# W_up by seven products, with each chain of added weight blocks spaced two products apart

## The chip, the cores and the metric

The kernel runs on one core of a Trainium2 chip. The metric is device time in microseconds, the median of several runs of the whole program. The engines that matter here: TensorE (PE) multiplies, VectorE (DVE) and ScalarE (ACT) work element by element, GpSimd (POOL) and SyncE (SP) issue transfers.

## The reference

Two layers of an encoder over 512 tokens of 1024 channels in fp32. The second half of each layer, which the change touches, is

```
h = RMSNorm(x)
x = x + W_down relu(W_up h)^2        W_up: 1024 x 4096, W_down: 4096 x 1024
```

The first half (four attention mixers, gates, an output projection "out") is not changed.

## The kernel before

Products are made to fp32 accuracy from pairs: every operand is split into a rounded `hi` (a cast on ACT, L215) and a remainder `lo` (a subtraction on DVE, L216), and three matmuls (hi x hi, hi x lo, lo x hi) are summed in PSUM. So each weight block, once it has landed, goes through a cast on ACT and a pass on DVE before PE can use it.

The MLP is done in four steps, j = 0 to 3, of 1024 hidden columns. `up` makes u = relu(W_up h)^2 for the step from chunks of 384, 384 and 256 columns, with all 512 tokens as moving columns. Only in the first chunk of j = 0 the tokens are taken in two halves of 256, so that the first half can begin when `norm` has only two of its four token tiles ready. `norm` works on tiles of 128 tokens: a root by Newton steps on [128 x 1] columns, two multiplications over 512 channels (`r_raw`), transposes on PE into PSUM banks (`tp`), and from there `h_hi` and `h_lo`.

For j = 0 to 2 W_down is multiplied by the Strassen-Winograd scheme (`add_product`): the operands are cut into 2 x 2 quarters, and seven products of sums of quarters take the place of eight. The sums of u's quarters (`left_sums`) are made on DVE. The sums of weight quarters (`right_sums`) are made by transfers that add into a block already loaded: SP loads `r_raw`, POOL issues a transfer that adds the next quarter from memory. One such block goes through a chain: split it, add to it, split it again. For j = 3 W_down is plain (`add_rows`), in column chunks of 256, 384 and 384, as "out" is.

The order on the engines is made as the program is built: `up` and `add_product` are generators that take turns, and a scheduler then orders each engine's instructions by its own estimates. On the chip each engine runs its list in order, and waits by semaphores. `NLEFT`, `NRIGHT` and `NSPLIT` are the numbers of buffers for the sums of u, for raw weight blocks, and for split ones. "Product 0 to 6" below are the seven products of a block in the order of the source.

Of the kernel before, what the change touches and what calls it, by code (L numbers as in the profile page):

```python
# [10 lines left out]
F32 = mybir.dt.float32  # L11
# [8 lines left out]
P = 128  # L20
S = 512
# [56 lines left out]
NLEFT, NRIGHT, NSPLIT = 8, 6, 2  # L78
# [86 lines left out]
class Net:  # L165
# [158 lines left out]
    def norm(self, pool, X, ms, g, tag="norm_h", bufs=2):  # L324
# [5 lines left out]
        for t in range(NT):  # L330
# [7 lines left out]
            for _ in range(3):  # L338
                stt(w, y, y, vh, op0=ALU.mult, op1=ALU.mult)
                stt(y, w, 1.5, y, op0=ALU.add, op1=ALU.mult)  # L340
            both = pool.tile([P, 2, S], F32, name=tag, tag=tag, bufs=bufs)
            for half in range(2):
                cs = slice(half * S, half * S + S)
                h = both[:, half, :]
                stt(h, X[t][:, cs], y, g[:, cs], op0=ALU.mult, op1=ALU.mult)
                ps = self.sps.tile([P, 4, P], F32, name="tp", tag="s")
                for j in range(4):
                    self.transpose(ps[:, j, :], h[:, j * P:(j + 1) * P])
                self.split(hi[:, half * 4:half * 4 + 4, t * P:(t + 1) * P],
                           lo[:, half * 4:half * 4 + 4, t * P:(t + 1) * P], ps)  # L350
        return hi, lo
# [752 lines left out]
    def up(self, pool, layer, j, u):  # L1104

        nc = self.nc
        for c0, w in self.col_chunks(0, D):
            units = self.chunk(layer, "up", 0, KD, [(j * D + c0, w)])
            tiles = [self.mm.tile([P, S], F32, name="mm", tag="mm") for _ in range(w // P)] if j == 0 and c0 == 0 else None
            if tiles:  # L1110

                for ts in (slice(0, S // 2), slice(S // 2, S)):
                    for f in range(w // P):
                        self.fm_group(tiles[f][:, ts], self.hT, units, f * P, ts)
            for f in range(0, w, P):
                ft = (c0 + f) // P
                if tiles:
                    ps = tiles[f // P]
                else:
                    ps = self.mm.tile([P, S], F32, name="mm", tag="mm")  # L1120
                    self.fm_group(ps, self.hT, units, f)
                r = pool.tile([P, S], F32, name="relu", tag="relu", bufs=2)
                nc.scalar.activation(r, ps, AF.Relu)
                nc.scalar.activation(u[:, ft, :], r, AF.Square)
                yield
# [8 lines left out]
    def left_split(self, pool, src):  # L1134
        hi, lo = (pool.tile([P, KD // 2, S // 2], F32R, name=x, tag="left", bufs=NLEFT) for x in ("l_hi", "l_lo"))
        self.split(hi, lo, src)
        return hi, lo

    def left_sums(self, pool, x, eng):

        h, kh = S // 2, KD // 2
        x11, x12, x21, x22 = x[:, 0:kh, 0:h], x[:, kh:, 0:h], x[:, 0:kh, h:], x[:, kh:, h:]

        put = lambda src: self.left_split(pool, src)

# [12 lines left out]
        yield put(x12)
        yield put(x22)

    def right_sums(self, pool, layer, name, k0):


        nc = self.nc
# [6 lines left out]
        source = lambda off: self.ins["wflat"][off:off + P * kk * n].rearrange("(p k n) -> p k n", p=P, k=kk)  # L1171

        def load(q):
            got = []
            for off in at[q]:
                raw = pool.tile([P, kk, n], F32, name="r_raw", tag="r_raw", bufs=NRIGHT)
                nc.sync.dma_start(raw, source(off))
                got.append(raw)
            return got

        def put(raws):
            got = []
            for raw in raws:
                hi = pool.tile([P, kk, n], F32R, name="r_hi", tag="r_hi", bufs=NSPLIT)
                lo = pool.tile([P, kk, n], F32R, name="r_lo", tag="r_lo", bufs=NSPLIT)
                self.split(hi, lo, raw)
                got += [(hi[:, k, :], lo[:, k, :]) for k in range(kk)]
            return got

        def add(to, q):  # L1190
            for raw, off in zip(to, at[q]):
                nc.gpsimd.dma_start(raw, source(off), accum_op=ALU.add)  # L1192
# [11 lines left out]
        yield put(load((1, 0)))  # L1204
        add(t, (1, 0))
        yield put(t)

    def add_product(self, pool, X, x, layer, name, k0):

        nc = self.nc  # L1210
        n = D // 2
        bank = {}

        def onto(t, nh, ps, op):
            x = X[t][:, nh * n:nh * n + n]
            nc.vector.tensor_tensor(x, x, ps, op=op)

        left, right = self.left_sums(pool, x, nc.vector), self.right_sums(pool, layer, name, k0)
        for p, ((hi, lo), w) in enumerate(zip(left, right)):

            if p in (0, 1):
                bank[p] = [self.sps.tile([P, S], F32, name="u", tag="s") for _ in range(2)]
            ps = bank[p % 2] if p < 5 else [self.mm.tile([P, S], F32, name="mm", tag="mm") for _ in range(2)]
            fresh = p in (0, 1, 5, 6)
            for k, (whi, wlo) in enumerate(w):
                first, end = fresh and k == 0, k == len(w) - 1
                for q in range(2):
                    toks = slice(q * P, (q + 1) * P)
                    for i, (a, b) in enumerate(((hi, whi), (hi, wlo), (lo, whi))):
                        nc.tensor.matmul(ps[q], a[:, k, toks], b, start=first and i == 0, stop=end and i == 2,  # L1230
                                         skip_group_check=True)
                        self.pe(n)
            for q in range(2):
                if p == 0:
                    onto(q, 0, ps[q], ALU.add)
                elif p == 1:
                    onto(2 + q, 1, ps[q], ALU.add)
                elif p == 2:
                    onto(q, 1, ps[q], ALU.subtract)
                elif p == 3:  # L1240
                    onto(q, 1, ps[q], ALU.add)
                elif p == 4:
                    onto(2 + q, 0, ps[q], ALU.add)
                    onto(2 + q, 1, ps[q], ALU.subtract)
                elif p == 5:
                    onto(q, 0, ps[q], ALU.add)
                else:
                    onto(2 + q, 0, ps[q], ALU.add)
            yield

    def run(self):
# [14 lines left out]
        for layer in range(self.depth):  # L1266
            act = self.attention(layer)
            last = layer == self.depth - 1
            with tc.tile_pool(name=f"mlp{layer}", bufs=1) as pool:
# [7 lines left out]
                self.hT = self.norm(pool, X, ms, g, "r_raw", NRIGHT)  # L1277
# [97 lines left out]
```

## Time and profile before

| | |
|---|---|
| median of 3 runs | 1854.19 us (1853.7 to 1855.83) |
| profiled execution | 1853.6 us, its span 1851.7 us, mean granted clock of TensorE 0.988 |
| PE busy | 1787.2 us, 97% of the span |
| DVE busy | 1201.0 us, 65% |
| ACT busy | 935.0 us, 50% |
| POOL busy | 419.0 us, 23% |

The rows below give times from the start of the span. PE's listed durations overlap, since matmuls are pipelined: what one costs is the distance between two starts. In layer 0 the MLP follows the last matmul of "out" at 596 us.

### The profile page before, as it was taken

How to read it: one execution, taken by the hardware profiler on the slowest of the kernel's cores; microseconds unless marked ns; L12 is line 12 of the kernel's file. 1: busy time of each engine (PE TensorE's matmuls, PEld its weight loads, DVE VectorE, ACT ScalarE, POOL GpSimd, SP SyncE). 2: the span in 40 equal slices, each digit the busy share in tenths (PEclk: the TensorE clock that was granted, in tenths of full speed). 3: DMA queues.
4: the chain of work that ended last, by engine and by line, in shares of the span. 5: the costliest groups of instructions: out<-in, count | busy, mean ns of one | idle time of the engine just before them, and what ended most of it. 6: DMA issues, size and time to landing. Idle time of an engine off the chain costs nothing.

```text
span 1851.7 us, 26873 instructions
## 1 busy us (share of the span) xinstructions
PE 1787.2 (97%) x9392; PEld 1556.9 (84%) x9392; DVE 1201.0 (65%) x2553; ACT 935.0 (50%) x1905; POOL 419.0 (23%) x1215
## 2 busy tenths in 40 slices
PE   6998999999999999999999989999999999999999
PEld 5897897887889888888999979887878898888889
DVE  6677876677665465655477878666876664565652
ACT  4565664555533454554346656645553345554541
POOL 2462254333010000010023604532422000010100
PEclk9999999999999999999999989999999999999999
DMA  4312123121324656564343211221222545565622
GB/s 164 115 53 68 60 73 93 44 69 56 90 83 154 207 124 166 129 156 105 96 153 98 76 61 52 79 72 60 73 66 73 159 151 134 149 153 165 138 82 89
DMA packets 73320, 193.91 MB, mean 105 GB/s; under 512 B 8928, under 2 KB 14048, under 8 KB 73184
## 3 DMA queue, kind: packets, MB, share of 16 engines
q1 hardware_dynamic: 66272, 167.02, 28.2%
q0 software_dynamic: 6912, 25.17, 8.0%
q8 instruction: 74, 1.21, 0.3%
q14 instruction: 62, 0.51, 0.1%
HBM read 187.97 MB, written 4.19 MB: 104 GB/s over the span
## 4 chain that ended last, share of the span: by engine, by line
PE 78%; DVE 8%; POOL 6%; issue 3%; ACT 2%; DMA 2%; SPq 1%; POOLq 0%; DVEq 0%; ACTq 0%
PE mm L285 19%; PE mm L286 19%; PE mm L287 19%; PE u L1230 9%; PE mm L1230 4%; PE tp L222 3%; PE s L604 2%; POOL rs_w_qk L235 2%; DVE w_lo L216 1%; POOL rs_y_qk L238 1%; POOL rs_w_qk L236 1%; POOL rs_w_qk L237 1%; PE y L631 1%; PE y L630 1%; DMA x<-in_x 1%
## 5 line engine op out<-in xcount | busy, mean ns | idle before, releaser
L285 PE MATMUL mm<-h_hi,w_hi 128*128 128x512 f32 (+1 forms) x1104 | 424.8, 386 | 1.8 <-DVE sig L1029 1.0
L286 PE MATMUL mm<-h_lo,w_hi 128*128 128x512 f32 (+1 forms) x1104 | 423.5, 385 | 1.7 <-DVE h_lo L216 1.4
L287 PE MATMUL mm<-h_hi,w_lo 128*128 128x512 f32 (+1 forms) x1104 | 419.6, 385 | 4.3 <-DVE w_lo L216 2.4
L216 DVE TENSOR_TENSOR w_lo<-w_raw,w_hi 128x768 fp32r<-128x768 f32 (+2 forms) x337 | 299.8, 899 | 158.5 <-ACT w_hi L215 157.1
L215 ACT CAST w_hi<-w_raw 128x768 fp32r<-128x768 f32 (+2 forms) x337 | 258.1, 774 | 232.2 <-PE mm L286 105.3
L287 PEld LDWEIGHTS mm<-h_hi,w_lo 128*128 128x128 f32 x1104 | 208.5, 189 | 44.7 <-DVE w_lo L216 3.9
L285 PEld LDWEIGHTS mm<-h_hi,w_hi 128*128 128x128 f32 x1104 | 208.6, 189 | 43.1 <-DVE sig L1029 2.9
L286 PEld LDWEIGHTS mm<-h_lo,w_hi 128*128 128x128 f32 x1104 | 209.0, 189 | 41.0 <-DVE h_lo L216 2.5
L287 PE MATMUL mm<-w_hi,h_lo 128*128 128x384 f32 (+1 forms) x576 | 190.0, 331 | 2.6 <-DVE h_lo L216 2.6
L286 PE MATMUL mm<-w_lo,h_hi 128*128 128x384 f32 (+1 forms) x576 | 189.7, 331 | 1.8 <-DVE w_lo L216 1.7
L285 PE MATMUL mm<-w_hi,h_hi 128*128 128x384 f32 (+1 forms) x576 | 189.2, 334 | 1.1 <-ACT w_hi L215 0.5
L216 DVE TENSOR_TENSOR r_lo<-r_raw,r_hi 128x1024 fp32r<-128x1024 f32 x84 | 102.7, 1223 | 130.3 <-ACT r_hi L215 130.3
L1192 POOL DMA_DIRECT2D r_raw<-in_wflat x48 | 41.6, 870 | 613.9 <-DVE r_lo L216 248.9
L235 POOL TENSOR_TENSOR rs_w_qk<-rs_y_qk 128x4 f32<-128x4 f32 (+2 forms) x216 | 61.8, 286 | 436.2 <-DVE rs_y_qk L233 300.0
L215 ACT CAST r_hi<-r_raw 128x1024 fp32r<-128x1024 f32 x84 | 88.3, 1051 | 69.2 <-PE u L1230 39.2
L286 PEld LDWEIGHTS mm<-w_lo,h_hi 128*128 128x128 f32 x576 | 110.4, 192 | 3.5 <-DVE w_lo L216 2.6
L287 PEld LDWEIGHTS mm<-w_hi,h_lo 128*128 128x128 f32 x576 | 110.1, 191 | 3.6 <-DVE h_lo L216 2.9
L285 PEld LDWEIGHTS mm<-w_hi,h_hi 128*128 128x128 f32 x576 | 110.1, 192 | 2.8 <-ACT h_hi L215 0.8
L216 DVE TENSOR_TENSOR pt_lo<-tp,pt_hi 128x256 fp32r<-128x256 f32 (+2 forms) x144 | 77.9, 552 | 39.6 <-ACT pt_hi L215 30.8
L215 ACT CAST pt_hi<-tp 128x256 fp32r<-128x256 f32 (+2 forms) x144 | 66.8, 478 | 66.4 <-PE tp L222 52.5
L1230 PE MATMUL u<-r_hi,l_lo 128*128 128x512 f32 x240 | 93.7, 390 | 0.0
L1230 PE MATMUL u<-r_lo,l_hi 128*128 128x512 f32 x240 | 93.5, 390 | 0.0
(192 smaller groups left out, 3602.5 us busy)
## 6 DMA issues: line engine op xcount, KB each, us to landing
w_raw<-in_wflat SPq DMA_DIRECT2D x248, 384.0 KB, 3.3
r_raw<-in_wflat SPq DMA_DIRECT2D x48, 512.0 KB, 3.6
r_raw<-in_wflat POOLq DMA_DIRECT2D x48, 512.0 KB, 5.8
w_raw<-in_wflat SPq DMA_DIRECT2D x88, 256.0 KB, 2.7
x<-in_x SPq DMA_DIRECT2D x8, 512.0 KB, 5.7
d_full<-in_mask_d SPq DMA_DIRECT2D x8, 448.0 KB, 4.5
x_save<-x SPq DMA_DIRECT2D x4, 512.0 KB, 4.5
x<-x_save SPq DMA_DIRECT2D x4, 512.0 KB, 5.5
```

Of the source, the lines that this page charges most:

```text
L215: self.nc.scalar.copy(hi, src)
L216: self.nc.vector.tensor_tensor(lo, src, hi.bitcast(F32), op=ALU.subtract)
L222: self.nc.tensor.transpose(out, in_, self.ident_r if short else self.ident)
L235: eng.tensor_tensor(w, y, y, op=ALU.mult)
L236: eng.tensor_tensor(w, w, v, op=ALU.mult)
L237: eng.tensor_scalar(w, w, -0.5, 1.5, op0=ALU.mult, op1=ALU.add)
L285: nc.tensor.matmul(ps, st[0], mv[0], start=first, stop=False)
L286: nc.tensor.matmul(ps, st[0], mv[1], start=False, stop=False)
L287: nc.tensor.matmul(ps, st[1], mv[0], start=False, stop=last)
L604: self.nc.tensor.matmul(ps, q[:, qc], k[:, kc], start=i == 0, stop=i == len(ks) - 1)
L1192: nc.gpsimd.dma_start(raw, source(off), accum_op=ALU.add)
L1230: nc.tensor.matmul(ps[q], a[:, k, toks], b, start=first and i == 0, stop=end and i == 2, skip_group_check=True)
```

## The change

W_up is multiplied by seven products too. The first 512 hidden columns are made plainly (`up_first`), all of them in two halves of 256 tokens and from `r_raw` blocks; the other seven blocks of 512 columns of a layer go through the new `up`: seven products of 24 matmuls, each with a stationary 128 x 128 and 256 moving columns. The sums of h's quarters are made once per layer (`row_sums`) from a copy of h that `norm` now keeps (`keep`, eight copies from PSUM on ACT). The sums of weight quarters of a block are one chain of three adding transfers, used in products 0, 2, 4 and 6, and one addition of two loaded blocks on DVE (`merge`). `right_sums` of W_down is put in the same form: three adding transfers for each half and a merge on DVE, in place of four transfers. POOL issues 78 such transfers instead of 48 in all.

u is held in quarter blocks of 4 x 256. `norm` works out the root of the next tile ahead of the transposes of this one. The last product of W_down takes two chunks of 512 columns, from `r_raw` blocks. PE has 10178 matmuls instead of 9314.

```diff
-NLEFT, NRIGHT, NSPLIT = 8, 6, 2
+NLEFT, NRIGHT, NSPLIT, NU = 6, 8, 4, 7
...
-        for t in range(NT):
+        y = inverse(0)
+        for t in range(NT):
             both = pool.tile([P, 2, S], F32, name=tag, tag=tag, bufs=bufs)
...
+            y = inverse(t + 1) if t + 1 < NT else None
+            banks = []
+            for half in range(2):
                 ps = self.sps.tile([P, 4, P], F32, name="tp", tag="s")
...
+            if keep is not None:
+                for half, ps in enumerate(banks):
+                    nc.scalar.copy(keep[half, t // 2][:, :, t % 2 * P:t % 2 * P + P], ps)
...
+    def split_block(self, pool, raw):
+        hi = pool.tile(list(raw.shape), F32R, name="r_hi", tag="r_hi", bufs=NSPLIT)
+        lo = pool.tile(list(raw.shape), F32R, name="r_lo", tag="r_lo", bufs=NSPLIT)
+        self.split(hi, lo, raw)
+        return [(hi[:, k, :], lo[:, k, :]) for k in range(raw.shape[1])]
+
+    def merge(self, to, raw):
+        self.nc.vector.tensor_tensor(to, to, raw, op=ALU.add)
...
+    def up_first(self, pool, layer, u):
+
+        units = self.plain_blocks(pool, layer, "up", 0, 0)
...
+        for f in range(4):
+            self.fm_group(tiles[f][:, early], self.hT, units, f * P, early)
+            self.squared_relu(u[0, 0][:, f, :], tiles[f][:, early])
...
+    def row_sums(self, pool, raw):
...
+        s1 = total(x21, x22, ALU.subtract)
+        hi, lo = (x[:, 0:kh, h:] for x in self.hT)
+        self.split(hi, lo, s1)
+        own = [(hi[:, k, :], lo[:, k, :]) for k in range(kh)]
+        s2 = total(s1, x11, ALU.subtract)
+        sums = [s2, total(x11, x21, ALU.subtract), total(s2, x12, ALU.add)]
...
+        def product(ps, left, raw, fresh):
+            right = self.split_block(pool, raw)
+            for f in range(2):
+                for k, (x, w) in enumerate(zip(left, right)):
+                    for i, (a, b) in enumerate(((1, 0), (0, 0), (0, 1))):
+                        nc.tensor.matmul(ps[:, f, :], w[a][:, f * P:(f + 1) * P], x[b], start=fresh and f + k + i == 0,
+                                         stop=k == kh - 1 and i == 2, skip_group_check=True)
...
+        t = load(0, 0)
+        a = bank()
+        product(a, x11, t, True)
+        add(t, 0, 1)
+        nc.scalar.copy(out[0, 0], a)
+        yield
+        c = bank()
+        product(c, x12, load(1, 0), True)
...
+        b = bank()
+        product(b, s1, t, True)
+        add(t, 1, 1)
+        nc.scalar.copy(out[1, 1], b)
+        t3, w22 = load(0, 1), load(1, 1)
+        self.merge(t3, w22)
+        yield
+        product(b, s4, w22, False)
...
+        product(a, s2, t, False)
+        add(t, 1, 0)
...
+        product(a, s3, t3, False)
...
+        product(a, x22, t, False)
...
         t = load((0, 0))
-        yield put(t)
+        got = put(t)
         add(t, (0, 1))
-        yield put(t)
+        yield got
+        yield put(load((1, 0)))
+        got = put(t)
         add(t, (1, 1))
-        yield put(t)
-        yield put(load((1, 1)))
-        t3 = load((0, 1))
-        add(t3, (1, 1))
+        yield got
+        t3, w22 = load((0, 1)), load((1, 1))
+        for a, b in zip(t3, w22):
+            self.merge(a, b)
+        yield put(w22)
...
+                        for i, _ in enumerate(self.up(pool, layer, j * D + c * S, u, c, sums)):
+                            if prev is not None and (i + c) % 2:
+                                next(prev, None)
```

Where instructions stand now, at three places. First PE at the norm of layer 0, behind the last matmuls of "out" (`m_hi`, `m_lo`); `tp` are the transposes, `mm<-h..` the first matmuls of W_up. Before:

```order
L287 MATMUL mm<-w_hi,m_lo 128x384
L222 MATMUL tp<-ident,r_raw 128x128 x16
L285 MATMUL mm<-h_hi,w_hi 128x256 x3
L286 MATMUL mm<-h_lo,w_hi 128x256
L287 MATMUL mm<-h_hi,w_lo 128x256
```

And now:

```order
L287 MATMUL mm<-w_hi,m_lo 128x384
L222 MATMUL tp<-ident,r_raw 128x128 x32
L285 MATMUL mm<-h_hi,r_hi 128x256
L286 MATMUL mm<-h_lo,r_hi 128x256
L285 MATMUL mm<-h_hi,r_hi 128x256
```

All 32 transposes stand ahead of W_up's first matmul; the other 16 stood among the matmuls before.

Second ACT at the same place. Before, the transposed banks of tiles 2 and 3 (the last four `h_hi`) with the first two raw blocks of W_down among them:

```order
L215 CAST h_hi_6903<-tp_6986 128x4x128
L215 CAST h_hi_6903<-tp_6994 128x4x128
L215 CAST r_hi_7465<-r_raw_7461 128x1024
L215 CAST h_hi_6903<-tp_7018 128x4x128
L215 CAST r_hi_7469<-r_raw_7463 128x1024
L215 CAST h_hi_6903<-tp_7026 128x4x128
```

And now, from the bank after tiles 0 and 1 on; `r_hi_7053` is the first weight block of W_up:

```order
L361 COPY h_raw_6903<-tp_6942 128x4x128
L361 COPY h_raw_6905<-tp_6949 128x4x128
L361 COPY h_raw_6903<-tp_6976 128x4x128
L215 CAST h_hi_6907<-tp_7010 128x4x128
L361 COPY h_raw_6905<-tp_6983 128x4x128
L215 CAST h_hi_6907<-tp_7017 128x4x128
L361 COPY h_raw_6904<-tp_7010 128x4x128
L361 COPY h_raw_6906<-tp_7017 128x4x128
L215 CAST h_hi_6907<-tp_7029 128x4x128
L215 CAST r_hi_7053<-r_raw_7051 128x1024
L215 CAST h_hi_6907<-tp_7036 128x4x128
```

Six copies stand ahead of the last tile's first `h_hi`, and the cast of W_up's first block stands behind that.

Third DVE in j = 0, after the first block of columns. `r_raw_7329` is the block of the chain of the second block (products 0, 2, 4, 6), `r_raw_7558` that of the third. Before, DVE had here the casts of plain chunks:

```order
L216 TENSOR_TENSOR w_lo_7218<-w_raw_7216,w_hi_7217 128x768
L216 TENSOR_TENSOR w_lo_7224<-w_raw_7222,w_hi_7223 128x768
L216 TENSOR_TENSOR w_lo_7230<-w_raw_7228,w_hi_7229 128x768
L216 TENSOR_TENSOR w_lo_7236<-w_raw_7234,w_hi_7235 128x768
L216 TENSOR_TENSOR w_lo_7326<-w_raw_7324,w_hi_7325 128x512
L216 TENSOR_TENSOR l_lo_7458<-u_7035,l_hi_7457 128x1024
```

And now:

```order
L216 TENSOR_TENSOR l_lo_7626<-u_7047,l_hi_7625 128x1024
L216 TENSOR_TENSOR r_lo_7333<-r_raw_7329,r_hi_7332 128x1024
L216 TENSOR_TENSOR r_lo_7366<-r_raw_7363,r_hi_7365 128x1024
L216 TENSOR_TENSOR h_lo_6908<-l_sum_7295,h_hi_6907 128x4x256
L216 TENSOR_TENSOR r_lo_7398<-r_raw_7329,r_hi_7397 128x1024
L216 TENSOR_TENSOR r_lo_7433<-r_raw_7429,r_hi_7432 128x1024
L1228 TENSOR_TENSOR u_7049<-u_7049,mm_7362 128x512
L216 TENSOR_TENSOR r_lo_7462<-r_raw_7329,r_hi_7461 128x1024
L1134 TENSOR_TENSOR r_raw_7702<-r_raw_7702,r_raw_7704 128x1024
L216 TENSOR_TENSOR r_lo_7494<-r_raw_7427,r_hi_7493 128x1024
L216 TENSOR_TENSOR r_lo_7525<-r_raw_7329,r_hi_7524 128x1024
L216 TENSOR_TENSOR r_lo_7562<-r_raw_7558,r_hi_7561 128x1024
```

Four splits of one block now stand in DVE's list with an adding transfer between each two, and the first split of the third block stands behind the last of them.

## Rows read from the trace of the kernel before

**Rows 1.** The page's busy times: engine, busy us, share of span, instructions.

```profile
PE 1787.2 (97%) x9392; PEld 1556.9 (84%) x9392; DVE 1201.0 (65%) x2553; ACT 935.0 (50%) x1905; POOL 419.0 (23%) x1215
```

**Rows 2.** Windows over the MLP of layer 0: length, busy us by engine, clock, transfers.

```profile
core 0: us, PE busy (x) PEld busy (x) DVE busy (x) ACT busy (x) POOL busy (x), PEclk, DMA share, GB/s
...
640.00:706.00 66.00, 66.00 (x292) 54.56 (x292) 40.08 (x43) 32.79 (x41) 3.45 (x4) 1.00 0.45 118
...
809.00:891.00 82.00, 82.00 (x362) 67.82 (x362) 48.67 (x53) 41.09 (x53) 3.45 (x4) 1.00 0.43 110
```

**Rows 3.** PE's timeline at 384 and 256 moving columns: start, us, instruction.

```profile
1505.79 0.33 PE L286 MATMUL mm<-w_lo,m_hi 128*128 128x384 f32 x1
...
1507.00 0.33 PE L287 MATMUL mm<-w_hi,m_lo 128*128 128x384 f32 x1
...
1511.10 0.28 PE L285 MATMUL mm<-h_hi,w_hi 128*128 128x256 f32 x1
...
1514.33 0.28 PE L285 MATMUL mm<-h_hi,w_hi 128*128 128x256 f32 x1
```

**Rows 4.** Timeline of the norm in layer 0, three engines.

```profile
596.03 1.91 PE L222 MATMUL tp<-ident,r_raw 128*128 128x128 f32 x16
...
596.66 2.05 ACT L215 CAST h_hi<-tp 128x512 fp32r<-128x512 f32 x4 [0.64 <-PE tp L222]
597.09 0.55 DVE L1096 TENSOR_TENSOR x<-x,mm 128x384 f32<-128x384 f32 x1
...
597.68 1.88 DVE L216 TENSOR_TENSOR h_lo<-tp,h_hi 128x512 fp32r<-128x512 f32 x3
...
598.28 0.61 PE L285 MATMUL mm<-h_hi,w_hi 128*128 128x256 f32 x3 [0.34 <-ACT h_hi L215]
...
599.61 0.39 PE L286 MATMUL mm<-h_lo,w_hi 128*128 128x256 f32 x1 [0.72 <-DVE h_lo L216]
...
603.56 0.22 DVE L339 SCALAR_TENSOR_TENSOR norm_w<-norm_y,norm_vh 128x1 f32<-128x1 f32 x1
...
604.01 1.42 DVE L345 SCALAR_TENSOR_TENSOR r_raw<-x,norm_y,norm_g 128x512 f32<-128x512 f32 x2
```

**Rows 5.** Groups by form, 600 to 891 us: busy us, mean ns, idle before.

```profile
L216 DVE TENSOR_TENSOR r_lo<-r_raw,r_hi 128x1024 fp32r<-128x1024 f32 x42 | 51.4, 1223 | 64.0 <-ACT r_hi L215 64.0
...
L215 ACT CAST r_hi<-r_raw 128x1024 fp32r<-128x1024 f32 x42 | 44.1, 1051 | 33.5 <-PE u L1230 18.3 <-PE mm L1230 13.0 <-DMA r_raw<-in_wflat 2.1
...
L1216 DVE TENSOR_TENSOR x<-x,u 128x512 f32<-128x512 f32 x36 | 23.4, 682 | 1.6 <-PE u L1230 1.5
```

**Rows 6.** Groups by form, 900 to 1500 us, at 256 columns.

```profile
L216 DVE TENSOR_TENSOR pt_lo<-tp,pt_hi 128x256 fp32r<-128x256 f32 x24 | 10.0, 418 | 2.1 <-ACT pt_hi L215 1.6 <-PE y L630 0.5
...
L215 ACT CAST pt_hi<-tp 128x256 fp32r<-128x256 f32 x24 | 8.9, 371 | 11.6 <-PE tp L222 7.7 <-PE y L631 3.8
```

**Rows 7.** Timeline of DVE and POOL at a link of W_down's chain.

```profile
659.07 1.22 DVE L216 TENSOR_TENSOR r_lo<-r_raw,r_hi 128x1024 fp32r<-128x1024 f32 x1
660.21 1.22 DVE L216 TENSOR_TENSOR l_lo<-l_sum,l_hi 128x1024 fp32r<-128x1024 f32 x1
...
660.59 0.86 POOL L1192 DMA_DIRECT2D r_raw<-in_wflat  x1 [0.87 <-DVE r_lo L216]
```

**Rows 8.** Transfers issued in 650 to 700 us, then in 608 to 640.

```profile
r_raw<-in_wflat POOLq DMA_DIRECT2D x4, 512.0 KB, 5.5
...
r_raw<-in_wflat POOLq DMA_DIRECT2D x4, 512.0 KB, 8.8
```

**Rows 9.** The page's queues: packets, MB, share of 16 engines' span.

```profile
q1 hardware_dynamic: 66272, 167.02, 28.2%
q0 software_dynamic: 6912, 25.17, 8.0%
```

**Rows 10.** A pause of PE in the attention of layer 0: timeline, then a window.

```profile
1068.72 1.29 PE L285 MATMUL mm<-y_hi,w_hi 128*128 128x512 f32 x2 [4.64 <-ACT y_hi L215]
...
1068.72:1072.50 3.78, 3.78 (x9) 2.90 (x10) 3.78 (x15) 1.45 (x3) 0.03 (x1) 0.50 0.23 85
```

More of the change, by code (lines that the diff above doesn't have):

```diff
@@ L1102, in add_rows @@
                     ms[t].append(part)
[L1104 to L1125, printed above, removed]
@@ L1211, in add_product @@
         n = D // 2
+        add, sub = ALU.add, ALU.subtract
+        steps = (("a", True, ((0, 0, add),)), ("c", True, ((0, 0, add),)), ("b", True, ((1, 1, add),)),
+                 ("b", False, ((0, 1, add),)), ("a", False, ((0, 1, sub),)),
+                 ("a", False, ((1, 0, add), (1, 1, sub))), ("c", True, ((1, 0, add),)))
         bank = {}
[L1214 to L1224, printed above, removed]
+        left, right = self.left_sums(pool, x), self.right_sums(pool, layer, name, k0)
+        for (hi, lo), w, (key, fresh, places) in zip(left, right, steps):
+            if fresh:
+                bank[key] = [self.sps.tile([P, S], F32, name="u", tag="s") for _ in range(2)]
+            ps = bank[key]
             for k, (whi, wlo) in enumerate(w):
-                first, end = fresh and k == 0, k == len(w) - 1
                 for q in range(2):
@@ L1229, in add_product @@
                     for i, (a, b) in enumerate(((hi, whi), (hi, wlo), (lo, whi))):
[L1230 to L1231 removed]
+                        nc.tensor.matmul(ps[q], a[:, k, toks], b, start=fresh and k + i == 0,
+                                         stop=k == len(w) - 1 and i == 2, skip_group_check=True)
                         self.pe(n)
[L1233 to L1248, printed above, removed]
+            for th, nh, op in places:
+                for q in range(2):
+                    to = X[2 * th + q][:, nh * n:nh * n + n]
+                    nc.vector.tensor_tensor(to, to, ps[q], op=op)
             yield
@@ L1281, in run @@
                 for j in range(4):
-                    u = pool.tile([P, KD, S], F32, name="u", tag="u", bufs=2)
-                    for i, _ in enumerate(self.up(pool, layer, j, u)):
-                        if prev is not None and (j < 3 or i):
-                            next(prev, None)
+                    u = self.blocks(pool, "u")
+                    if j == 0:
+                        self.up_first(pool, layer, u)
+                        sums = self.row_sums(pool, raw)
+                    for c in range(1 if j == 0 else 0, 2):
+                        for i, _ in enumerate(self.up(pool, layer, j * D + c * S, u, c, sums)):
+                            if prev is not None and (i + c) % 2:
+                                next(prev, None)
                     if j < 3:
```

146 lines of the change are left out of this document (105 added, 41 removed).

## The prediction

> **What bounds the kernel now.** I read the page's busy times first: TensorE works 1787.2 of 1851.7 us, 97% [rows 1], so the end is set by the sum of its work and the few places where it waits. The windows over the MLP come next: in 640 to 706 us it is busy all 66.0 us, in 809 to 891 all 82.0, while VectorE has 61% and 59% of these stretches and ScalarE about 50% [rows 2]. There is nothing to be won in the body of the MLP but fewer or shorter matmuls; and any wait that the change brings shows in full.
>
> The price of a matmul is its spacing, not its listed duration. With 512 moving columns, 82.0 us hold 362 [rows 2]: 0.2265 us. With 256, from 1511.10 to 1514.33 there are 27 steps: 0.1196; with 384, from 1505.79 to 1507.00, seven: 0.173 [rows 3].
>
> The timeline of the norm in layer 0 comes third. After the last matmul of "out" PE makes the 16 transposes of token tiles 0 and 1, and at 598.28 begins on W_up for these 256 tokens, with waits of 0.34 and 0.72 us [rows 4]. The norm of tiles 2 and 3 is worked out under these matmuls. Layer 1 shows the same.
>
> **Term 1, TensorE's work.** Seven of the eight blocks of 512 hidden columns change from 96 matmuls of 512 (96 x 0.2265 = 21.75) to 7 products of 24 matmuls of 256 (168 x 0.1196 = 20.09): -1.65. The saving of an eighth in columns comes out as less than 8% in time, since a 256-column matmul costs more than half of a 512 one. Over 7 blocks and 2 layers: -23.1. The last product of W_down in each layer goes from column chunks of 256, 384, 384 (96 matmuls each: 11.5 + 16.6 + 16.6 = 44.7) to 192 of 512 (43.5): -1.2, twice -2.4. The first block runs in halves throughout (192 x 0.1196 = 23.0 against 17.2 + 5.4 = 22.6): +0.3, twice +0.6. W_down's other products keep their number and their size. Sum -24.9.
>
> Here the Trainium skill is more generous than the rows. TensorE: Matmul & The Clock Gate, Back-to-back issue gap, gives for a single stream N/2.4 + 2.5 ns, 109 ns for 256 columns and 216 for 512; by that an estimate for a block is 18.3 against 20.7 us, and the total would come out some 10 us lower than below. The rows show the two sizes next to this very work, and are taken.
>
> **Term 2, from the norm to the first steady product.** PE's order now has all 32 transposes ahead of the first matmul of W_up, so that matmul waits for the whole norm. I walk layer 0 on the axis of the old trace, since the order up to there is the same.
>
> The last matmul of "out" ends at 596.2. The addition to x for tile 3 then takes 0.55 (596.9; the w_lo casts that delayed it before are gone), two steps of tile 2's root 0.45, its two multiplications 1.42 [rows 4]: 598.7. VectorE next makes six h_lo at 0.63 each (1.88 for three) and six root steps of tile 3, about 0.23 each (603.56 to 604.01 is two) [rows 4]: 5.2 us, and loses about 0.4 because ScalarE now has a copy of h to write for each transposed bank, each behind the h_lo of that bank: 604.3. Half of the multiplications 0.7, four transposes 0.5 (1.91 for 16), h_hi 0.59 [rows 4], and r_hi of the first block, which stands behind it on ScalarE, 1.05 [rows 5]: the first matmul at 607.1, against 598.28.
>
> PE has then 192 matmuls of 256 for the first block, and behind them the products 0, 1, 2, 4, 3 of the second block, before the first product of the third. With no wait that is 37.3 us. VectorE is the one to follow. From 606.1 it has in its order 2 h_lo, 4 r_lo, 4 sums of rows of h, 10 w_lo of 256 columns, a merge, an l_lo and the r_lo of product 0: eleven passes over 1024 columns at 1.14 (659.07 to 660.21 [rows 7]), ten at some 0.4 (0.418 [rows 6]), two at 0.63: 17.8 us. The casts that they follow on ScalarE (0.371 for 256 columns [rows 6]) cost some 1.8 more. r_lo of product 0 is done at 625.7.
>
> From here a chain decides: r_lo, an adding transfer into the same block, r_hi, r_lo. A link in the old trace: r_lo at 659.07 + 1.22, the transfer is issued at 660.59 [rows 7], so 0.3; 5.5 to landing where little else moves [rows 8]; 1.05 and 1.22 for the casts [rows 5]; 8.15 with 0.1 for signals. Little covers it: one product (2.9 us) stands between the uses of the block in products 0 and 2 and none between 2 and 4, because W_down has no product to put there yet. Three links end at 650.2, and behind the third r_lo stands, in VectorE's order, the r_lo for the third block's first product: 651.3. PE begins that product at 651.3. In the old scheme the same work without waits would be reached at 598.28 + 1.1 for the later half of the transposes and the old waits beside them at 0.7 + 0.9, that is 638.4 with its 37.3. So 12.9 per layer, twice +25.8. The bounds: casts at their closest spacing and a link at 7.7 give 10.5 per layer; transfers that land in 8.8 us, as they did where queues were full [rows 8], give 3 x 3.3 more, 22.
>
> **Term 3, the steady part, j = 1 to 3.** PE has 336 matmuls of 256 and 168 of 512: 78.2 us per j. VectorE's passes come to 43 of 1024 columns and 22 of 512 (0.68 [rows 5]): 52.6 + 15 = 67.6 by durations, 64 by spacing: 82 to 86%, against 60% now. The DMA engines: q1 moved 167.02 MB in 28.2% of the span, 1.64 us per block of 512 KB, q0 its 48 additions in 8.0%, 3.1 each [rows 9]; 16 loads and 12 additions per j are 63 of 78 us, 81%. Neither is full, and with W_down's products between those of W_up a link of 8.15 lies under two to four products (5.7 to 14 us). Walking one period in the order of the engines, I find covers of 0.2 us (second half of W_down's third product, whose load waits for an r_lo), 0.7, 1.4 and one of -0.3. I take 1 us per j, between 0 and 4: +6 for six j (0 to +24).
>
> Costed at nothing: the merges (counted in VectorE's load; 1.2 us each on the chain if VectorE should be full), the copies into the output banks (ScalarE at 62%), the u quarter blocks, and the clock. As for the clock: where PE stood still from 1064.1 to 1068.7, the granted clock went to 0.50 (the 1.2 GHz level), and was still there until 1072.5, with 0.42 us per matmul of 512 [rows 10]. The gap of the norm may do the same, which costs up to 1.9 us in the first block, but PE then waits that much less for the chain behind it.
>
> **Sum.** -24.9 + 25.8 + 6 = +6.9 on the profiled execution's 1853.6: 1860.5. The three runs' median lies 0.6 above it: 1861.
>
> **The rivals.**
> Faster. The waits of term 2 stay near 8 us per layer and the steady part has none: -25 + 16 = -9: 1845. For it: VectorE's 17.8 us between the norm and r_lo of product 0 hold most of the delay, and would be shorter if its passes ran closer than in the rows. Against it: three links of transfers are latency, and nothing lies between them. It decides where all new waits fall below 21 us, 10.6 per layer.
> No change to be measured (a run's spread makes 0.2%, 3.7 us, the limit). The walk holds, at its shorter bound, and term 3 is nought to 4: -25 + 22 + 2 = -1: 1853.
> The steady part runs into VectorE or the transfers. For it: 82 to 86% and 81% of load, additions that took 8.8 us to land at 608 to 640 [rows 8]. At 3.3 us more per link and three uncovered links per j, of which half lies in the covers: 5 us per j, 30 in all, on the top of the rest: 1885. Against it: loads go out up to eight blocks ahead.
> The product scheme on W_up gives nothing: a block at 7/8 of the columns but 1.75 times the matmuls would have to space at 0.1295; the 27 steps say 0.1196, so I give that no chance of its own.
>
> **Chances.** My forecast (1858 to 1872) 0.40, the steady part bound (1872 to 1895) 0.18, no change 0.18, faster 0.24. So faster 0.24, same 0.18, slower 0.58. The range leaves out the far ends of the first and the last: 1843 to 1882; the likeliest case alone has 1857 to 1870.
>
> **What would show it.** Matmuls of 256 in W_up at 0.12 us. At each norm a gap on PE of about 7 us besides the transposes, with a granted clock below 1 behind it. Then two waits of 2 to 4 us, both put down to r_lo on VectorE, the second ahead of the third block's first product, and additions on POOL 8 us apart. From then to the end of the layer PE busy to 98% or more, VectorE near 80%. I am wrong in term 2 if the first matmul of W_up begins before 604 or the third block's first product before 647; wrong in term 3 if PE's waits on r_lo come to more than 4 us per j.

## The result

The changed kernel takes 1865.91 us (median of 4 runs, 1864.41 to 1869.67) against 1853.95 for the kernel before in the same measurement: ratio 1.0066, interval 1.0048 to 1.0083. It is slower, as forecast, by 12 us where 7 were forecast; the span of the profiled execution went from 1851.7 to 1862.6 us.

The page's busy times and PE's timeline and windows say where. First the page's busy times after the change (they answer to [rows 1]):

```profile
PE 1772.7 (95%) x10256; PEld 1577.2 (85%) x10256; DVE 1320.9 (71%) x2645; ACT 1010.2 (54%) x1999; POOL 445.2 (24%) x1245
```

PE has 864 matmuls more than before (10256 against 9392 in the traces) and is busy 14.5 us less, yet the span is 10.9 us longer: its idle time grew by 25.4 us. PE's busy time also hides matmuls at half clock, as will be seen.

Next come rows of PE's timeline at the norm of layer 0 (start, us, instruction; they answer to [rows 4]):

```profile
596.94 1.91 PE L222 MATMUL tp<-ident,r_raw 128*128 128x128 f32 x16
600.74 1.33 PE L222 MATMUL tp<-ident,r_raw 128*128 128x128 f32 x8 [1.89 <-ACT h_raw L361]
605.40 1.94 PE L222 MATMUL tp<-ident,r_raw 128*128 128x128 f32 x8 [3.33 <-DVE r_raw L349]
608.10 0.58 PE L285 MATMUL mm<-h_hi,r_hi 128*128 128x256 f32 x1 [0.77 <-ACT r_hi L215]
608.48 0.41 PE L286 MATMUL mm<-h_lo,r_hi 128*128 128x256 f32 x1
608.69 0.41 PE L285 MATMUL mm<-h_hi,r_hi 128*128 128x256 f32 x1
```

W_up begins 11.2 us after the first transpose; before it was 2.25. Three waits stand in between: for a copy of h on ACT (it reads the PSUM bank that the next transposes need), for the last tile's multiplication, and for the cast of the first weight block. The last two matmuls start 0.21 us apart, where 0.12 is the spacing at full clock [rows 3]: half clock, as the windows below show.

After that the chain of adding transfers, in the timelines of ACT, DVE, POOL and PE:

```profile
626.37 1.05 ACT L215 CAST r_hi<-r_raw 128x1024 fp32r<-128x1024 f32 x1 [2.20 <-PE mm_y L286]
627.45 1.23 DVE L216 TENSOR_TENSOR r_lo<-r_raw,r_hi 128x1024 fp32r<-128x1024 f32 x1 [2.03 <-ACT r_hi L215]
629.30 1.02 POOL L1125 DMA_DIRECT2D r_raw<-in_wflat  x1 [110.67 <-DVE r_lo L216]
636.39 1.05 ACT L215 CAST r_hi<-r_raw 128x1024 fp32r<-128x1024 f32 x1 [3.94 <-DMA r_raw<-in_wflat]
639.01 0.87 POOL L1125 DMA_DIRECT2D r_raw<-in_wflat  x1 [8.68 <-DVE r_lo L216]
646.69 0.58 PE L1215 MATMUL mm<-w_hi,r_lo 128*128 128x256 f32 x1 [4.71 <-DVE r_lo L216]
646.93 0.85 POOL L1125 DMA_DIRECT2D r_raw<-in_wflat  x1 [7.06 <-DVE r_lo L216]
655.97 0.38 PE L1215 MATMUL mm<-h_hi,r_lo 128*128 128x256 f32 x1 [1.49 <-DVE r_lo L216]
656.21 0.87 POOL L1125 DMA_DIRECT2D r_raw<-in_wflat  x1 [8.43 <-DVE r_lo L216]
```

POOL's transfers stand 9.7, 7.9 and 9.3 us apart (the last is the next chain's first), and PE waits twice for an r_lo, 4.71 and 1.49 us. ACT's first row shows a wait that the forecast did not have: the cast of product 0's block waits 2.20 us for PE, which still reads the first block from the split buffers. Layer 1 has the same two waits:

```profile
1560.46 0.39 PE L1215 MATMUL mm<-w_hi,r_lo 128*128 128x256 f32 x1 [3.42 <-DVE r_lo L216]
1569.70 0.58 PE L1215 MATMUL mm<-h_hi,r_lo 128*128 128x256 f32 x1 [3.28 <-DVE r_lo L216]
```

The windows (busy us by engine, granted clock, share of the transfer engines; answers to [rows 2, 10]) give the clock behind these gaps, and the steady part:

```profile
606.00:608.00 2.00, 1.34 (x7) 0.93 (x5) 0.69 (x1) 1.48 (x3) 0.00 (x0) 0.50 0.57 121
612.00:616.00 4.00, 4.00 (x31) 4.00 (x31) 4.00 (x5) 0.54 (x2) 0.00 (x0) 0.84 1.03 423
644.00:646.00 2.00, 0.00 (x0) 0.00 (x0) 0.59 (x1) 1.67 (x2) 0.00 (x0) 0.50 0.47 193
650.00:652.00 2.00, 2.00 (x16) 2.00 (x15) 0.00 (x0) 0.00 (x0) 0.00 (x0) 0.79 0.95 197
...
660.00:740.00 80.00, 80.00 (x517) 72.87 (x516) 65.09 (x68) 49.97 (x60) 10.35 (x12) 1.00 0.77 182
740.00:820.00 80.00, 79.97 (x514) 72.64 (x513) 64.10 (x66) 48.33 (x58) 10.53 (x13) 1.00 0.79 187
820.00:890.00 70.00, 70.00 (x455) 64.03 (x454) 56.77 (x58) 45.40 (x55) 9.31 (x11) 1.00 0.83 198
```

From 660 us on PE does not wait at all, with VectorE at 81% and the transfer engines at 77 to 83%. So what the change loses, it loses in some 60 us between the norm and the third block.

### The profile page after: what moved, and what is told of

Same layout as the page of the kernel before. It is cut to its first block, busy times and chain, and to the rows that moved or that the text cites. A ratio compares the mean times of both kernels' runs of the same rounds, so it can differ in the third digit from the quotient of the medians.

```text
span 1862.6 us, 28777 instructions
## 1 busy us (share of the span) xinstructions
PE 1772.7 (95%) x10256; PEld 1577.2 (85%) x10256; DVE 1320.9 (71%) x2645; ACT 1010.2 (54%) x1999; POOL 445.2 (24%) x1245
## 4 chain that ended last, share of the span: by engine, by line
PE 74%; DVE 8%; POOL 7%; issue 4%; DMA 3%; ACT 2%; SPq 0%; POOLq 0%; DVEq 0%; ACTq 0%
PE mm L1215 14%; PE mm L285 14%; PE mm L286 13%; PE mm L287 13%; PE u L1344 12%; PE tp L222 3%; DMA r_raw<-in_wflat 2%; POOL rs_w_qk L235 2%; PE s L615 2%; POOL rs_w_qk L236 1%; POOL rs_w_qk L237 1%; POOL rs_y_qk L238 1%; PE y L642 1%; PE y L641 1%; DVE w_lo L216 1%
## 5 line engine op out<-in xcount | busy, mean ns | idle before, releaser
L216 DVE TENSOR_TENSOR r_lo<-r_raw,r_hi 128x1024 fp32r<-128x1024 f32 x206 | 250.8, 1221 | 101.1 <-ACT r_hi L215 99.4
L215 ACT CAST r_hi<-r_raw 128x1024 fp32r<-128x1024 f32 x206 | 215.7, 1050 | 128.7 <-PE mm L1215 47.9
L285 PE MATMUL mm<-h_hi,w_hi 128*128 128x512 f32 x544 | 217.9, 401 | 1.1 <-DVE sig L1040 1.0
L287 PE MATMUL mm<-h_hi,w_lo 128*128 128x512 f32 x544 | 214.4, 400 | 4.4 <-DVE w_lo L216 2.5
L286 PE MATMUL mm<-h_lo,w_hi 128*128 128x512 f32 x544 | 215.7, 397 | 0.0
L1215 PE MATMUL mm<-h_hi,r_lo 128*128 128x256 f32 x448 | 127.2, 284 | 4.8 <-DVE r_lo L216 4.8
L1215 PE MATMUL mm<-h_lo,r_hi 128*128 128x256 f32 x448 | 128.2, 286 | 0.0
L1215 PE MATMUL mm<-h_hi,r_hi 128*128 128x256 f32 x448 | 128.0, 286 | 0.0
L1344 PE MATMUL u<-r_hi,l_hi 128*128 128x512 f32 x336 | 126.2, 390 | 0.0
L286 PEld LDWEIGHTS mm<-h_lo,w_hi 128*128 128x128 f32 x544 | 103.5, 190 | 20.5
```

What stands on the lines that cost most here:

```text
L215: self.nc.scalar.copy(hi, src)
L216: self.nc.vector.tensor_tensor(lo, src, hi.bitcast(F32), op=ALU.subtract)
L285: nc.tensor.matmul(ps, st[0], mv[0], start=first, stop=False)
L286: nc.tensor.matmul(ps, st[0], mv[1], start=False, stop=False)
L287: nc.tensor.matmul(ps, st[1], mv[0], start=False, stop=last)
L1215: nc.tensor.matmul(ps[:, f, :], w[a][:, f * P:(f + 1) * P], x[b], start=fresh and f + k + i == 0, stop=k == kh - 1 and i == 2, skip_group_ ...
```

## The experiments

The attention phases of these runs, which no experiment touches, differ from profile to profile: what is left of the span without the MLPs and "out" lies between 1071.6 us (before) and 1076.9 (e10). The table therefore also has the MLPs by themselves, from PE's timeline: from the first transpose of the MLP's norm to that of the next norm (layer 0) or to the end (layer 1), summed; and "out", the two output projections, from their first matmul to the MLP's first transpose. Each ratio is to runs of the kernel before in the same measurement, whose medians lay between 1853.95 and 1855.53.

| kernel | median us | ratio to before, 95% interval | MLPs us | "out" us |
|---|---|---|---|---|
| before | 1853.95 | | 685.4 | 94.8 |
| after | 1865.91 | 1.0066 (1.0048 to 1.0083) | 695.4 | 94.4 |
| e1_own_sums | 1850.24 | 0.9976 (0.9967 to 0.9985) | 679.0 | 94.7 |
| e2_early_split | 1851.93 | 0.9979 (0.9970 to 0.9989) | 675.0 | 97.8 |
| e3_both | 1839.12 | 0.9913 (0.9897 to 0.9930) | 663.4 | 98.6 |
| e4_own_sums_more | 1849.92 | 0.9967 (0.9954 to 0.9980) | 678.7 | 94.5 |
| e5_kept_busy | 1861.70 | 1.0040 (1.0025 to 1.0055) | 691.7 | 94.7 |
| e6_kept_less_busy | 1863.31 | 1.0045 (1.0027 to 1.0062) | 697.6 | 94.6 |
| e7_split_in_norm | 1840.87 | 0.9926 (0.9910 to 0.9943) | 669.2 | 94.6 |
| e8_second_block_plain | 1855.97 | 0.9997 (0.9986 to 1.0007) | 683.0 | 96.9 |
| e9_split_one_two | 1839.81 | 0.9917 (0.9904 to 0.9930) | 669.5 | 94.5 |
| e10_split_two_late | 1838.84 | 0.9911 (0.9899 to 0.9924) | 667.1 | 94.3 |
| e11_kept_busy_again | 1863.06 | 1.0048 (1.0036 to 1.0061) | 691.4 | 94.5 |
| e12_kept_less_busy_again | 1865.48 | 1.0057 (1.0045 to 1.0069) | 695.6 | 94.5 |

**e1, the chain on VectorE.** The four weight quarters of the second block (`own` is `j == 0`) are loaded once, and the sums made by `merge`:

```diff
         t = load(0, 0)
+        if own:
+            w = {(1, 0): load(1, 0), (0, 1): load(0, 1), (1, 1): load(1, 1)}
+            load = lambda r, c: w[r, c]
+            add = lambda raw, r, c: self.merge(raw, w[r, c])
         a = bank()
```

> The chain of the second block (j = 0) without adding transfers: its four weight quarters are loaded once and added on VectorE; all else as after the change. Theory A (the forecast's term 2: a chain of transfers is what PE waits for there): the waits on r_lo of 4.7 and 1.5 us vanish, and with them the half clock behind the longer one (some 2.2 us), 8.4 per layer: 1849 us. Rival B (VectorE's list is what limits, the transfers lie beside it): with three more passes on VectorE the wait only moves, 1862 us or more.

1850.24 us, theory A's figure within 1.3; the MLPs lost 16.4 us, 8.2 per layer against 8.4 expected. The list of PE's waits in layer 0 up to 900 us has only those of the norm left:

```profile
PE tp L222 <- DVE r_raw L349: 3.3, 1, 3.3
PE tp L222 <- ACT h_raw L361: 1.9, 1, 1.9
PE mm L285 <- ACT r_hi L215: 0.8, 1, 0.8
```

In layer 1 one wait on r_lo of 1.1 us is left, ahead of the third block's first product. Nothing of the size of rival B appears, and it falls: VectorE had room for three more passes just there, and what PE waited for was the transfers' latency.

**e2, the first weight blocks split early.**

```diff
                 raw = self.blocks(pool, "h_raw")
+                units = self.plain_blocks(pool, layer, "up", 0, 0)
                 self.hT = self.norm(pool, X, ms, g, "r_raw", NRIGHT, raw)
...
-                        self.up_first(pool, layer, u)
+                        self.up_first(pool, layer, u, units)
```

> The first weight blocks of W_up are split ahead of the norm in the program, so that PE's matmuls for the first 256 tokens stand between the transposes again; all else as after the change. Theory A: PE starts near 600 us instead of 608, without half clock; the chain begins some 5 us earlier because four r_lo have left VectorE's list behind the norm: 4 to 6 us per layer, 1854 to 1858 us. Rival B (the gap of the norm is swallowed by the chain behind it, which hangs on the last tile's h and not on PE): 0 to 2 per layer, 1862 to 1866 us.

1851.93 us, below even theory A's range. PE's timeline at the norm has W_up's matmuls between the transposes again, with no wait above 0.84 us, and the two waits of the chain are still there:

```profile
598.36 1.91 PE L222 MATMUL tp<-ident,r_raw 128*128 128x128 f32 x16
601.11 0.62 PE L285 MATMUL mm<-h_hi,r_hi 128*128 128x256 f32 x3 [0.84 <-ACT h_hi L215]
602.16 0.66 PE L222 MATMUL tp<-ident,r_raw 128*128 128x128 f32 x4 [0.32 <-ACT h_raw L361]
...
638.16 0.58 PE L1214 MATMUL mm<-w_hi,r_lo 128*128 128x256 f32 x1 [2.91 <-DVE r_lo L216]
...
647.36 0.39 PE L1214 MATMUL mm<-h_hi,r_lo 128*128 128x256 f32 x1 [0.53 <-DVE r_lo L216]
...
1546.61 0.39 PE L1214 MATMUL mm<-w_hi,r_lo 128*128 128x256 f32 x1 [2.02 <-DVE r_lo L216]
...
1555.91 0.58 PE L1214 MATMUL mm<-h_hi,r_lo 128*128 128x256 f32 x1 [3.33 <-DVE r_lo L216]
```

In layer 0 both are shorter than after the change (4.71 and 1.49), in layer 1 only the first is (3.42 and 3.28).

The chain's first transfer was issued 23.4 us after the first transpose (621.74 on POOL) and not 32.4 (629.30 after 596.94): 9 us earlier where I expected 5. Four r_lo (4.6 us) have left VectorE's list, and PE, which started early and at full clock, gives up the split buffers sooner: ACT's cast of product 0's block now waits 1.06 us for it, not 2.20. Rival B, that the gap is swallowed by the chain, falls. The price stands in the table's last column: the four casts now come ahead of the projection's weight casts, 3.4 us over both layers.

**e3, both.**

> The two edits of e1 and e2 together. Theory A: the gains add and what e2 alone could not show comes out, 8.4 and 8 to 10 per layer: 1829 to 1835 us. Rival B: after e1 PE waits for VectorE's list instead, so that the gap's time stays: about 1845 us.

1839.12 us, 0.9913 of before: faster than both kernels. The gains add, though not quite (MLPs -16.4 and -20.4, together -32.0 of 36.8): with the early split a part of the chain's wait was gone already. Rival B falls. The whole run missed theory A's 1829 to 1835 by the 4 us lost in "out", which I had not counted. What PE still waits for in layer 0 up to 900 us (layer 1 has the same rows, with 1.5 in place of 0.6):

```profile
PE mm L285 <- ACT h_hi L215: 0.8, 1, 0.8
PE mm L1214 <- DVE r_lo L216: 0.6, 1, 0.6
PE tp L222 <- ACT h_raw L361: 0.3, 1, 0.3
```

**e4, four of seven blocks on VectorE.** As e1, with `own` for `j == 0 or c == 0`.

> As e1, and in j = 1 to 3 the first of the two blocks of each step also adds its weight quarters on VectorE: three more passes of 1.14 us and three transfers fewer per step, VectorE at some 91% of the steady part. Theory A (the steady part has slack on VectorE): within 4 us of e1, 1847 to 1853 us. Rival C (VectorE is near its limit there, as the second rival of the forecast had it): 2 us or more per step, 1861 us or more.

1849.92 us, no different from e1. The window says why: VectorE rises from 81 to 86% (the 91% expected started from the forecast's 86) and the transfer engines fall from 0.77 to 0.70, and PE still does not wait. In the windows that follow, up to 890 us and in layer 1, it waits 0.3 us each at most.

```profile
660.00:740.00 80.00, 80.00 (x519) 73.14 (x518) 68.77 (x70) 48.63 (x58) 7.79 (x9) 1.00 0.70 167
```

Rival C, and with it the forecast's rival of a steady part at its limit, falls at this load.

**e5 and e6, e11 and e12, the clock.** Matmuls that nobody reads, on operands of the tile just normed, keep PE busy in the norm: 4 behind tile 1 and 11 behind tile 2, in the control (e6, e12) 1 and 3.

```diff
                 banks.append(ps)
+            if keep is not None and t:
+                ps = self.mm.tile([P, S], F32, name="idle", tag="mm")
+                cs = slice(t * P, t * P + P)
+                for _ in range((0, 4, 11, 0)[t]):
+                    nc.tensor.matmul(ps, hi[:, 0, cs], hi[:, 0:4, cs], start=True, stop=True)
```

> As after the change, with 4 and 11 matmuls of 512 columns, whose results nobody reads, put between the transposes of the norm where PE stood idle (0.9 and 2.5 us of work), to see what the lower granted clock behind the norm costs. Theory D (PE at half clock holds the split buffers of the first block longer, and with them the start of the chain of adds): first block of W_up at full clock, r_lo of product 0 some 2 us earlier, 1861 to 1862 us, and 2 us per layer below the run with fewer such matmuls. The forecast's own entry (the clock costs nothing, since PE then waits less for the chain): 1865 to 1867 us and no difference between the two.

> The control to e5: the same edit with 1 and 3 such matmuls, so that the scheduler's lists on VectorE are the same in layer 0, and PE is idle for most of the norm. Theory D: granted clock at half behind the norm as after the change, 1865 to 1866 us. The forecast's entry: no difference from e5.

In layer 0 the granted clock did what was wanted. In 608 to 612 us, where the first block runs, first e5, then e6:

```profile
608.00:612.00 4.00, 3.52 (x27) 3.32 (x28) 3.75 (x5) 4.00 (x6) 0.00 (x0) 1.00 0.90 337
```

```profile
608.00:612.00 4.00, 4.00 (x22) 4.00 (x22) 4.00 (x4) 3.42 (x5) 0.00 (x0) 0.55 1.01 393
```

In layer 1 of e5 it was not quite so: there the clock was at 0.50 from 1524.4 to 1527.8 us, within the first block. POOL's issues of the chain's first transfer and of the next chain's, in both layers, again first e5, then e6:

```profile
628.76 1.02 POOL L1130 DMA_DIRECT2D r_raw<-in_wflat  x1 [110.12 <-DVE r_lo L216]
...
654.72 0.87 POOL L1130 DMA_DIRECT2D r_raw<-in_wflat  x1 [8.48 <-DVE r_lo L216]
...
1544.08 0.89 POOL L1130 DMA_DIRECT2D r_raw<-in_wflat  x1 [110.13 <-DVE r_lo L216]
...
1569.92 0.86 POOL L1130 DMA_DIRECT2D r_raw<-in_wflat  x1 [8.39 <-DVE r_lo L216]
```

```profile
627.95 1.02 POOL L1130 DMA_DIRECT2D r_raw<-in_wflat  x1 [110.77 <-DVE r_lo L216]
...
653.78 0.87 POOL L1130 DMA_DIRECT2D r_raw<-in_wflat  x1 [8.66 <-DVE r_lo L216]
...
1546.75 0.89 POOL L1130 DMA_DIRECT2D r_raw<-in_wflat  x1 [110.77 <-DVE r_lo L216]
...
1573.53 0.86 POOL L1130 DMA_DIRECT2D r_raw<-in_wflat  x1 [9.57 <-DVE r_lo L216]
```

Counted from layer 0's first transpose (597.07 and 595.64) they stand at 31.7 and 57.7 in e5 and at 32.3 and 58.1 in e6, and in e11 and e12 they stand at 32.4 and 58.0, and 32.2 and 57.7: the chain ends at the same place within 0.4 us, whatever the clock behind the norm, and theory D's mechanism does not show. In layer 1 (from 1512.13 and 1513.98) they stand at 32.0 and 57.8 in e5, and at 32.8 and 59.5 in e6; e11 and e12 have 31.6 and 57.8, and 32.6 and 59.4. There the controls start the chain 0.8 and 1.0 us later, half of what theory D named, and lose 1.2 and 1.3 us more since their third transfer landed after 6.7 and 6.8 us and not 5.5. No run says why it did.

What differs in both layers is where the clock falls next. In layer 0 of e5 it is at 0.50 in 644 to 648 us and full again before the second wait, so PE would have waited for the second r_lo anyway; in e6 it is still full there and falls at the second wait:

```profile
652.00:656.00 4.00, 2.46 (x11) 2.47 (x12) 3.21 (x4) 3.29 (x6) 0.87 (x1) 0.57 0.57 150
656.00:660.00 4.00, 4.00 (x23) 4.00 (x22) 1.23 (x1) 0.48 (x1) 0.00 (x0) 0.58 0.92 245
```

The same two kernels again:

> e5 again with more rounds, beside its control on the same chip. In the profiles of e5 and e6 the two MLPs together took 5.9 us less where PE was kept busy; the medians of the whole runs differed by 1.6 with ranges that overlap. Theory D: 3 to 6 us below e12. The forecast's entry: no difference.

> The control e6 again with more rounds. Theory D: 3 to 6 us above e11. The forecast's entry: no difference.

2.4 us apart, after 1.6 the first time; the intervals of the ratios overlap both times, so the times of the whole runs do not tell a cost from none. The MLPs of the profiles are 5.9 and 4.2 us apart. In e5 and e11 the clock is full behind the second wait in both layers; in e6 and e12 it is at 0.50 there, for 9.2 and 6.7 us of work over both layers. At 0.213 us a matmul in place of 0.119 that is an estimate of 4.1 and 3.0 us, and the third transfer's late landing of 1.2 and 1.3 fills most of the rest. So a low clock costs where it falls behind the last wait, some 3 to 4 us over both layers by this estimate, and not by the way that theory D named; the size is not shown beyond that.

**e7, e9, e10, a better place for the early split.** In e7 all four blocks are split within the norm behind token tile 1; in e9 one ahead of the norm and three behind tile 1; in e10 two ahead and two behind tile 2. All have the chain of e1. The diff is that of e10; `make` splits the blocks that are left.

```diff
+                units = self.plain_blocks(pool, layer, "up", 0, 0, (0, 2))
...
                 banks.append(ps)
+            if make is not None and t == 2:
+                units += make()
```

> As e3 (own sums, early split), with the split of W_up's first block put into the norm behind token tile 1 in place of ahead of the norm. Theory A (e3 lost some 2 us per layer in the output projection, because four casts stood ahead of its weight casts, and its MLP had no wait left to speak of): the output projection back at 47.3 us, 1834 to 1836 us. Rival: the casts now stand ahead of the tile's own h_hi and delay the norm by as much, 1838 to 1840 us.

> As e7, but one of the four weight blocks of the first product of W_up is split ahead of the norm and three within it, behind token tile 1, so that PE has one block when tiles 0 and 1 are there and the output projection loses one cast's time at most. Theory: projection 47.5 to 48 us and MLP near e3's, 1835 to 1838 us. Rival: the three casts still stand ahead of h_hi of tiles 2 and 3 and the norm stays as late as in e7, 1839 to 1842 us.

> Two of the four weight blocks split ahead of the norm, two behind token tile 2. Theory: PE has work for the 256 early tokens from the start and the tiles' own casts come first in the norm, but two casts stand in the projection (+1): 1835 to 1838 us. Rival: as for e9, 1839 to 1842 us.

1840.87, 1839.81 and 1838.84 us: the projection is back at 94.3 to 94.6, 4.0 to 4.3 us below e3, and the MLPs lose 5.8, 6.1 and 3.7 against e3. In e7 PE's timeline has a new wait for an h_lo; one of the four casts stands ahead of its h_hi on ACT, one of their passes ahead of it on DVE:

```profile
602.45 0.58 PE L286 MATMUL mm<-h_lo,r_hi 128*128 128x256 f32 x1 [1.98 <-DVE h_lo L216]
```

Behind this wait, which e9 has too, the granted clock was at 0.50 for 3.4 us in each layer of e7 and e9 (602.0 to 605.4 in e7's layer 0); in e3 and e10 it stayed at 1.00 through the norm. So the rivals were right for e7 (0.9 us above its range) and e9, and e10 ended between the two, no better than e3. My reading is that the four casts take some 4 us of ScalarE and 5 of VectorE (1.05 and 1.22 each) wherever they are put in these 60 us; how much of the loss in e7 and e9 is the clock was not tried.

**e8, the second block plain.** Its seven products are replaced by `plain_blocks` and 96 matmuls of 512 columns, ahead of `row_sums`:

```diff
+    def up_second(self, pool, layer, u):
+        units = self.plain_blocks(pool, layer, "up", 0, S)
+        for f in range(4):
+            ps = self.mm.tile([P, S], F32, name="mm", tag="mm")
+            self.fm_group(ps, self.hT, units, f * P)
...
-                    for c in range(1 if j == 0 else 0, 2):
+                    for c in range(2 if j == 0 else 0, 2):
```

> As after the change, but the second block of W_up's columns (j = 0) plain as well, 96 matmuls of 512 columns in place of seven products: no chain of adds before W_down's products are there to stand between. Theory A: the waits of 4.7 and 1.5 us and the half clock behind them (8.4) go, 1.65 us of PE's work come back: 6.7 per layer, about 1852 us. Rival: the chain of the third block now meets the same lack of cover, the wait moves there, 1860 us or more.

The MLPs lost 12.4 us, 6.2 per layer against 6.7, so theory A holds for the MLP; the whole run, 1855.97, is 4 us above its figure, since "out" took 2.5 us longer in this profile (layer 1) and the attention phase 1.6, which I cannot explain. The rival falls: in layer 0 the only wait left behind the norm is 0.6 us, and in layer 1 there is none.

```profile
PE u L1352 <- DVE r_lo L216: 0.6, 1, 0.6
```

The third block's chain has W_down's products beside it, and they cover it.

## Why the prediction was right, and where its terms were off

**Term 1 (-24.9) held.** In the changed kernel's first block 37 steps from 617.50 to 621.89 are 0.1186 us each, against 0.1196 in [rows 3]. e3, with 4.4 us of waits left in the MLPs against 2.1 before, has MLPs 22.0 us shorter than before, which leaves about -24 for the matmuls. The formula for the isolated spacing in Back-to-back issue gap, of TensorE: Matmul & The Clock Gate of the Trainium skill, makes it an estimate of 109 ns, 8% below the 118.6 ns measured here; the measurement decides.

**Term 2 (+25.8) had the right places and was too small.** The order of events came as walked: no start for W_up before the last tile (11.2 us after the first transpose, 11.1 forecast), r_lo of product 0, three links, two waits on r_lo (4.71 and 1.49 us in layer 0, 3.42 and 3.28 in layer 1, where 2 to 4 were forecast), the second ahead of the third block's first product. The forecast put that product 55.3 us after the first transpose (651.3 less 596.0); PE got there at 59.0 in layer 0 and 57.5 in layer 1. Its place for the same work without waits, 42.4 (638.4 less 596.0), is borne out: e3, with little left to wait for, got there at 43.2 and 44.1. One size was off, and one transfer was slow:

- The chain's start. "r_lo of product 0 is done at 625.7" left out that r_hi has four buffers and that the first block holds all four until PE is through with them. ACT waited 2.2 and 2.1 us for PE there, and POOL issued the first transfer 32.4 and 32.0 us after the first transpose where the walk has 30.0. The four runs e5, e6, e11 and e12 have the same chain and issued it at 31.6 to 32.8. No run had more split buffers, so that they are the cause is read from ACT's wait and not shown by a change.
- The first link in layer 0. "5.5 to landing where little else moves": the first transfer was issued at 629.30 and the cast that waited for it began at 636.39, 7.1 us later, so the link took 9.7 us, not 8.15. The other links took 7.9 to 8.4, and the same first transfer landed after 5.7 us in layer 1 and after 5.3 to 5.7 in e5, e6, e11 and e12. A block of 512 KB was being loaded beside it each time, so that alone does not explain it, and the cause stays open. The 5.5 of the forecast was sound; this is the scatter of one profile.

Both together are 3.8 us in layer 0 and, nearly all of it the chain's start, 2.2 in layer 1. e1 takes the chain away (-16.4 us in the MLPs), e2 the gap, and with it 9 us of the chain's start (-20.4), e3 both (-32.0). That is more than the 25.8 of the term; with 6.0 for these two, 2.7 for the clock in layer 1 (next paragraph), and 2.3 off for the waits that e3 has more than the kernel before, the sum is 32.2.

**The clock, "costed at nothing", was half right.** Behind the norm's gap the granted clock was at 0.50 from 603.0 to 613.3 us, and in layer 0 that cost nothing to speak of, as forecast: e5 and e6 end the chain at the same place, within 0.4 us. In layer 1 up to 1 us of it may have come through. But the chain's own waits can bring the clock down again, which I had not seen, and behind the second of them there is no further wait to take the loss. In the changed kernel's layer 1 it is so:

```profile
1566.00:1570.00 4.00, 0.72 (x5) 0.52 (x4) 2.71 (x3) 3.42 (x4) 0.06 (x1) 0.88 0.39 115
1570.00:1574.00 4.00, 4.00 (x20) 4.00 (x20) 2.61 (x3) 2.31 (x3) 0.80 (x1) 0.50 0.84 197
1574.00:1576.00 2.00, 2.00 (x12) 2.00 (x12) 0.00 (x0) 0.00 (x0) 0.00 (x0) 0.54 1.03 309
```

Twenty matmuls in 4 us where full clock passes 33: by these rows an estimate of 2.2 us over 1570 to 1576, and 2.7 from the end of the wait at 1569.70 on. In layer 0 the clock fell at the first wait and was full again at the second. Layer 1's MLP is 5.8 us longer than before, layer 0's 4.2, though its chain ended 1.5 us earlier.

**Term 3 (+6) was nought.** PE waited 0.2 us in all six steps. VectorE had 80 to 83%, at the lower end of the 82 to 86 forecast, and the transfer engines 77 to 83%, as forecast. The covers of 0.2 and -0.3 us that I found by hand were not that thin; e4 shows that even 86% leaves room. The rival of a steady part at its limit had too large a chance.

**The sum.** Per layer -12.45 for term 1 and nothing for term 3; the MLPs' +4.2 and +5.8 leave 16.7 and 18.3 for term 2, against 12.9. What term 3 did not take, 6 us over both layers, covered most of the 9.2 that term 2 was short. That the total came within 5 us is in part this offset, which was luck. Two slips in the forecast's bounds changed nothing: twice the shorter bound of 10.5 is 21, not 22, and 12.9 with three links 3.3 us longer is 22.8, not 22.

## What to carry to other kernels

A scheme that saves matmuls pays where its operands are made beside other work, and its cost sits at its ends: look first for the stretch in which there is nothing yet to put between the links of a chain (here the second block, before W_down has products), and there give up the cheap way of making sums (adding transfers, 8 us a link) for the one with short latency (VectorE, some 3.5 us a link: 1.22 for the pass, 1.05 and 1.22 for the split), even if it is the busier engine elsewhere. A change in which buffers the first operands come from can move their casts in an order, and the last tile of a norm then holds up all of PE; splitting the first weights ahead of the norm brought 14 us. When walking a chain by hand, walk the buffers too: who still holds the slot that the next step writes.

## What the runs showed of the hardware that was not expected

- PE's waits within a stream of matmuls brought the granted clock down to 0.50 (the 1.2 GHz level) at some places and not at others, and their length alone does not tell which. In the changed kernel it fell during the wait of 4.71 us that ended at 646.69 and was full again at 650.8; it fell during the wait of 3.28 us that ended at 1569.70 and was full again at 1575.8. It stayed at 1.00 behind the wait of 1.49 us that ended at 655.97, and also behind that of 3.42 us that ended at 1560.46 (1.00 in 1562 to 1566).
- In the norm, with 16 transposes between 600.7 and 607.3 and waits of 1.89 and 3.33 us among them, the clock was at 0.50 from 603.0 on. With 4 and 11 matmuls of 512 columns beside them it stayed at 1.00 up to the chain's first wait in layer 0 of e5 and layer 1 of e11; in the other layer of each it fell all the same, later (at 1524.4 in e5, at 611.3 in e11).
- An adding transfer of 512 KB took 5.3 to 5.8 us from issue to landing in 26 of the 30 links of this chain in the changed kernel, e5, e6, e11 and e12, with one block loaded beside it, and 6.1, 6.7, 6.8 and 7.1 us in the other four with the same beside it. The kernel before had 5.5 and 8.8 as medians of four [rows 8].
